# First stage of a transformer encoder layer: k stored once, q stores moved to SyncE's queue, four weight pieces loaded into buffers of h, late adaLN loads on GpSimd's queue, another order of the second chunk's tiles

## The chip, the cores and the metric

The kernel runs on one core of one Trainium2 chip. The metric is the device time of one execution in microseconds; the time of a kernel is the median of several executions. The profile is one more execution, taken by the hardware profiler. Engines are called PE (TensorE, matmuls), DVE (VectorE), ACT (ScalarE), POOL (GpSimd) and SP (SyncE, which only issues transfers here). ACT, POOL and SP can each issue DMAs; an issue stands in that engine's instruction order, and a DMA that waits for something holds up what follows on its engine.

## The reference

One encoder layer (depth 1) over 2048 tokens of width 1024, in float32: windowed attention with 16 query heads over 4 key/value heads of 64, then a gated feed-forward block of width 2816, each between two RMS norms with a conditioning vector c that gives shifts, scales and gates.

```python
mod = (silu(c) @ ada_w[i] + ada_b[i])[:, None, :]
sh1, sc1, g1, sh2, sc2, g2 = jnp.split(mod, 6, axis=-1)
h = rmsnorm(x, mix_norm_pre[i]) * (1.0 + sc1) + sh1
y = windowed_gqa_sink(h, att_w_qkv[j], att_w_o[j], att_sink[j], rel_bias)   # window of 128 to both sides
x = x + g1 * rmsnorm(y, mix_norm_post[i])
h = rmsnorm(x, ffn_norm_pre[i]) * (1.0 + sc2) + sh2
y = swiglu(h, ffn_w_in[i], ffn_w_out[i])
x = x + g2 * rmsnorm(y, ffn_norm_post[i])
```

The first stage, which the change is about, computes `mod`, `h` and the first half of the projection `qkv = h @ w_qkv`.

## The kernel before

**Precision.** A float32 product is made of three matmuls over halves: every operand is split into a high half (ACT: a cast to the matmul type) and a low half (DVE or POOL: operand minus high half), `split`, L149, and `three`, L143, multiplies high by high (L145), high by low (L146) and low by high (L147). So every tile that TensorE reads has two producers, and the second is often the later one.

**Chunks and tiles.** The 2048 tokens are four chunks of 512 (c = 0 to 3). The width of 1024 is eight slices of 128 (k = 0 to 7). The projection has twelve output tiles of 128 columns: 0 to 7 are q (two per key/value head), 8 and 9 are k, 10 and 11 are v, which is computed turned round (`v_tile`, psv). The weight's columns are stored in the order `NORD = [8, 9, 0, 1, 2, 3, 4, 10, 11, 5, 6, 7]`; the first seven (`WAVE`) are the first piece of each slice, `w0_k` (448 KB, loaded as wqkvk_0), the others the second piece, `w1_k` (320 KB, wqkvk_1). Low halves of first pieces are made by DVE, of second pieces by POOL.

**Chunk 0.** TensorE fills its start with 38 matmuls that nobody reads (`keep_busy`). The squares of x are summed over k (`squares0`), the sum over partitions is a matmul with ones (nst), and the inverse root goes to `normed`. Then comes the *first wave*: for every slice k two adaLN columns are loaded and reduced on DVE (`ada_reduce`, L297, a 128x1024 multiply-and-sum: scale 8+k and shift k), the first weight piece is split, x is scaled (L207), and h0_k is made: high half on ACT (L214), low half on DVE (L215). Both need the shift. Seven matmul groups over w0_k follow. Then the tiles are evacuated (`evac`, L219), the second pieces are loaded, and the *second wave* of chunk 0 computes tiles 10, 11, 5, 6, 7.

**Chunks 1 to 3.** Chunk 1 is computed after that, tile by tile, over the second pieces first and the first pieces last. Its squares are summed alternately on POOL and DVE (L186), its norm matmul takes the sum split into halves (L125, L126, in a buffer of the pool `ev`). Between the tiles stand the 24 late adaLN columns (16 to 39; `late_ada`): a load on SP's queue into one of four buffers `raws`, and a reduce on DVE. Chunks 2 and 3 are projected during attention, as *fillers*: a generator (`fill_qkv`) gives one slice of a tile at a time, loads its weights again (wsr), splits them on ACT and POOL (ws), and is asked for a measured amount (`FILL`) after each attention unit.

**Stores and loads.** Every finished q pair is stored in DRAM as four transfers of rows of 256 bytes (q_d, L235; issued by ACT for chunks 0 and 1, by SP for 2 and 3), k twice, once for each half of the partitions (k_d, L243), v once. Attention loads them per chunk and head (`load_qkv`, L457): q, k and v tiles from a pool that lies where the weight pieces were, so that a load waits for the last matmul that reads them.

**Attention.** A unit is 128 queries of one key/value head, four query heads at once, 64 units in all. `scores` (L483): two matmuls for each of four strips (s, L498), then on DVE the bias and the maximum (L501, writes pr and nm), on ACT the exponential with its sum (L503), on DVE a reciprocal (rs, L505), on POOL the scaling (L507). `values` (L513), two units later: transposes of pr (t, L520), split on ACT and DVE (phi, plo), products with v (L525, L526) and the sum of two halves (of, L530). The three buffers pr are cleared once by POOL (L448).

**Who sets the order.** Pools give each tile a buffer and make its next user wait for the readers of the last (`reuse_waits="tile"`). The order of instructions on each engine is set by a scheduler that simulates the program; `tc.issue_after(x)` tells it not to issue what follows before x. The engines then run their own instructions strictly in that order.

## Time and profile before

| | |
|---|---|
| median of 3 runs | 2087.45 us (2087.05 to 2092.54) |
| the profiled execution's own time | 2086.54 us |
| its span on the core | 2084.7 us |
| granted TensorE clock, mean | 0.986 |
| TensorE busy | 2011.4 us, 96% of the span |
| VectorE, ScalarE, GpSimd busy | 1505.5, 994.7, 912.5 us |
| TensorE busy from 0 to 100, 100 to 200 us | 74.2, 87.5 us |
| TensorE busy from 200 to 300 us | 96.41 us |

The span begins with the first and ends with the last instruction of the execution; 1.84 us lie around it. In a row of a timeline the bracket names the idle time of the engine before the instruction and what released it. A wait for several things is put down to the one that came last. The first stage ends at 199 us, with the first scores; attention and its fillers run to about 800 us, the feed-forward block from there to the end.

### The profile page before, as it was taken

How to read it: one execution, taken by the hardware profiler on the slowest of the kernel's cores; microseconds unless marked ns; L12 is line 12 of the kernel's file. 1: busy time of each engine (PE TensorE's matmuls, PEld its weight loads, DVE VectorE, ACT ScalarE, POOL GpSimd, SP SyncE). 2: the span in 40 equal slices, each digit the busy share in tenths (PEclk: the TensorE clock that was granted, in tenths of full speed). 3: DMA queues.
4: the chain of work that ended last, by engine and by line, in shares of the span. 5: the costliest groups of instructions: out<-in, count | busy, mean ns of one | idle time of the engine just before them, and what ended most of it. 6: DMA issues, size and time to landing. Idle time of an engine off the chain costs nothing.

```text
span 2084.7 us, 28731 instructions
## 1 busy us (share of the span) xinstructions
PE 2011.4 (96%) x9416; PEld 1660.3 (80%) x9416; DVE 1505.5 (72%) x2629; ACT 994.7 (48%) x2105; POOL 912.5 (44%) x894
## 2 busy tenths in 40 slices
PE   8698999999999998999999999999999999999998
PEld 5576787888888786888888887888888788888886
DVE  7376677677777668566576698787876598887656
ACT  4233677777777756333333353434433544453222
POOL 0412456543446536455666455545553333344300
PEclk9899999999999999999999999999999999999999
DMA  8699668665556665433643454544533454488763
GB/s 313 194 284 289 199 190 254 177 168 179 179 175 211 206 230 202 141 121 122 228 171 113 154 183 152 198 156 144 200 137 142 161 174 145 156 307 339 258 251 122
DMA packets 257285, 402.69 MB, mean 193 GB/s; under 512 B 84661, under 2 KB 135397, under 8 KB 255088
## 3 DMA queue, kind: packets, MB, share of 16 engines
q1 hardware_dynamic: 216592, 371.41, 52.9%
q10 hardware_dynamic: 39072, 25.18, 3.9%
q0 software_dynamic: 1472, 4.27, 0.5%
q8 instruction: 74, 1.21, 0.2%
q14 instruction: 75, 0.61, 0.1%
HBM read 267.83 MB, written 132.95 MB: 192 GB/s over the span
## 4 chain that ended last, share of the span: by engine, by line
PE 42%; DVE 4%; DMA 1%; issue 1%; POOL 1%; ACT 1%; SPq 0%; DVEq 0%; ACTq 0%; POOLq 0%
PE pc_i L145 8%; PE pc_i L147 8%; PE pc_i L146 8%; PE po L1205 5%; PE po L1206 5%; PE po L1204 5%; DVE z L1245 1%; PE pl L1229 1%; PE pl L1227 1%; PE pl L1228 1%; DMA wiri<-w_in 0%; DVE z L1249 0%; DMA ht<-hd_d_t 0%; DVE z L1209 0%; DVE wo_s L151 0%
## 5 line engine op out<-in xcount | busy, mean ns | idle before, releaser
L146 PE MATMUL pc_i<-ht,ws_i 128*128 128x512 f32 x528 | 207.1, 392 | 1.6 <-DVE ht L151 1.6
L145 PE MATMUL pc_i<-ht,ws_i 128*128 128x512 f32 x528 | 206.2, 391 | 1.8 <-ACT ht L150 1.7
L147 PE MATMUL pc_i<-ht,ws_i 128*128 128x512 f32 x528 | 206.8, 392 | 0.0
L150 ACT CAST wa_i<-wiri 128x512 fp32r<-128x512 f32 x132 | 81.7, 620 | 218.3 <-DMA wiri<-w_in 115.3
L507 POOL TENSOR_SCALAR pr<-pr,rs 128x288 f32<-128x288 f32 (+3 forms) x256 | 126.4, 514 | 116.3 <-DVE rs L505 106.5
L501 DVE CUSTOM_DVE_ANT_0 pr<-s,bias,nsink 128x288 f32<-128x288 f32 (+3 forms) x256 | 124.2, 500 | 57.5 <-PE s L498 47.3
L503 ACT ACTIVATE pr<-pr,nm 128x289 f32<-128x289 f32 (+3 forms) x256 | 135.3, 531 | 55.9 <-DVE nm L501 54.3
L879 POOL TENSOR_TENSOR s_i<-wiri 128x512 f32<-128x512 f32 x44 | 63.9, 1453 | 193.4 <-DMA wiri<-w_in 176.3
L151 DVE TENSOR_TENSOR wa_i<-wiri,wa_i 128x512 fp32r<-128x512 f32 x132 | 127.9, 969 | 22.3 <-ACT wa_i L150 22.0
L151 DVE TENSOR_TENSOR ws_i<-s_i,ws_i 128x512 fp32r<-128x512 f32 x132 | 125.4, 950 | 22.0 <-ACT ws_i L150 21.8
L1209 DVE TENSOR_TENSOR z<-po,z 128x512 f32<-128x512 f32 x164 | 110.6, 684 | 42.2 <-PE po L1206 40.4
L145 PE MATMUL pc_i<-hb,wa_i 128*128 128x512 f32 x352 | 138.1, 392 | 0.0
L147 PE MATMUL pc_i<-hb,wa_i 128*128 128x512 f32 x352 | 137.7, 391 | 0.0
L151 DVE TENSOR_TENSOR plo<-t,phi 128x512 fp32r<-128x512 f32 x184 | 121.9, 683 | 21.9 <-ACT phi L150 21.7
L146 PE MATMUL pc_i<-hb,wa_i 128*128 128x512 f32 x352 | 137.5, 391 | 0.0
L1204 PE MATMUL po<-wo_s,g 128*128 128x512 f32 x320 | 124.8, 393 | 2.0 <-DVE z L1209 1.4
L498 PE MATMUL s<-k,q 128*128 128x288 f32 (+4 forms) x512 | 110.0, 313 | 16.7 <-DMA k<-k_d 10.4
L1205 PE MATMUL po<-wo_s,g 128*128 128x512 f32 x320 | 125.4, 392 | 0.1
L1206 PE MATMUL po<-wo_s,g 128*128 128x512 f32 x320 | 125.2, 391 | 0.0
L520 PE MATMUL t<-ident,pr 128*128 128x128 f32 x736 | 116.0, 274 | 3.1 <-POOL pr L507 2.7
L145 PEld LDWEIGHTS pc_i<-ht,ws_i 128*128 128x128 f32 x528 | 99.5, 188 | 24.1 <-ACT ht L150 2.2
L146 PEld LDWEIGHTS pc_i<-ht,ws_i 128*128 128x128 f32 x528 | 99.5, 188 | 23.6 <-DVE ht L151 2.1
(251 smaller groups left out, 5907.2 us busy)
## 6 DMA issues: line engine op xcount, KB each, us to landing
wiri<-w_in SPq DMA_DIRECT2D x88, 512.0 KB, 4.7
ada<-ada_w SPq DMA_DIRECT2D x40, 512.0 KB, 6.4
wr<-w_out SPq DMA_DIRECT2D x20, 1024.0 KB, 9.1
g<-g_d_t SPq DMA_DIRECT2D x36, 512.0 KB, 5.2
g<-g_d_b SPq DMA_DIRECT2D x35, 512.0 KB, 5.7
q<-q_d SPq DMA_DIRECT2D x16, 1024.0 KB, 6.6
wsr<-w_qkv SPq DMA_DIRECT2D x24, 512.0 KB, 5.7
g<-g_d_t SPq DMA_DIRECT2D x44, 256.0 KB, 3.0
```

The costliest lines, as they stand in the source:

```text
L145: pe.matmul(ps, w[0], h[0], start=first, stop=False)
L146: pe.matmul(ps, w[0], h[1], start=False, stop=False)
L147: pe.matmul(ps, w[1], h[0], start=False, stop=last)
L151: return eng.tensor_tensor(lo, src, f(hi), ALU.subtract).ins
L501: dve.tensor_tensor_reduce(pr[:, i, lo:hi], ps[:, :n], bias[g][:, lo - starts[i]:hi - starts[i]], -1.0, nsink[:, g:g + 1], ALU.add, ALU.mi ...
L503: act.activation(pr[:, i, lo:hi + 1], pr[:, i, lo:hi + 1], AF.Exp, bias=nm[:, i:i + 1], scale=-1.0, accum_out=rs[:, i:i + 1])
L507: pool.tensor_scalar(pr[:, i, lo:hi], pr[:, i, lo:hi], rs[:, i:i + 1], 1.0, ALU.mult, ALU.mult)
L520: pe.transpose(pt[:, i * P:(i + 1) * P], pr[:, i, jj * P:(jj + 1) * P], ident)
L1204: pe.matmul(ps, g[:, 0], w[:, 0], start=i < FRESH and k == 0, stop=False, **on)
L1205: pe.matmul(ps, g[:, 0], w[:, 1], start=False, stop=False, **on)
L1206: pe.matmul(ps, g[:, 1], w[:, 0], start=False, stop=k == m - 1, **on)
L1209: dve.tensor_tensor(y, ps, y, ALU.add)
```

## The change

1. **k is stored once.** A k_d tile has 64 partitions instead of 128 and one store instead of two; `load_qkv` reads it twice, once into each half of the partitions, for the chunk itself and for the neighbours' edges.
2. **q stores of chunks 0 and 1 are issued by SP**, not by ACT.
3. **Four second weight pieces** (k = 0 to 3) are loaded into buffers of the pool `hs`, which holds the h tiles, rather than into `raws`; pool `w2` is opened ahead of `raws`.
4. **The late adaLN columns are loaded on GpSimd's queue**, three per tile of chunk 1 rather than two.
5. **Norms.** The squares of chunk 0 are summed to two tiles rather than four ahead of the matmul; chunk 1's norm takes its sum directly (one matmul, no halves) and is asked for after the first tile of the second wave rather than the second.
6. **First wave.** The reduce of the shift column of slice k is issued after the low half of h0_(k−1).
7. **Chunk 1's tiles** are computed in the order of NORD (8, 9, 0, 1, 2, 3, 4, 10, 11, 5, 6, 7), first pieces first, rather than with the second pieces first. Chunk 2's squares are summed on DVE alone.

```diff
     q_d = [[dram.tile([P, JB * GRP, P], F32, name=f"q_d{c}_{g}") for g in range(KVH)] for c in range(NCH)]
-    k_d = [[dram.tile([P, 2, CH], F32, name=f"k_d{c}_{g}") for g in range(KVH)] for c in range(NCH)]
+    k_d = [[dram.tile([DH, 2, CH], F32, name=f"k_d{c}_{g}") for g in range(KVH)] for c in range(NCH)]
     v_d = [[dram.tile([P, JB, P], F32, name=f"v_d{c}_{g}") for g in range(KVH)] for c in range(NCH)]
...
                     dve.tensor_tensor(sq[k - 1], sq[k - 1], sq[k], ALU.add)
-            self.acc = sq[::2]
-
-        def norm(self, psp, ptag):
-            self.r = rstd_of(lambda name: square_at(), psp, ptag, self.acc, f"a{self.c}", normed[:, 3])
+                if k % 4 == 3:
+                    dve.tensor_tensor(sq[k - 3], sq[k - 3], sq[k - 1], ALU.add)
+            self.acc = sq[::4]
+
+        def norm(self, psp, ptag, direct=False):
+            self.r = rstd_of(lambda name: square_at(), psp, ptag, self.acc, f"a{self.c}", normed[:, 3], direct)
         def h(self, k):
...
                     for i in range(2):
-                        (act if c < 2 else sp).dma_start(q_d[c][g][i * DH:(i + 1) * DH, :, 2 * j * QW:2 * (j + 1) * QW],
+                        sp.dma_start(q_d[c][g][i * DH:(i + 1) * DH, :, 2 * j * QW:2 * (j + 1) * QW],
                                      f(t[j * DH:(j + 1) * DH, i]).rearrange("p b e r -> p b (e r)"))
...
             for j in range(2):
-                for d in range(2):
-                    sp.dma_start(k_d[c][2 * (n - KT) + j][d * DH:(d + 1) * DH], f(t[j * DH:(j + 1) * DH]))
+                sp.dma_start(k_d[c][2 * (n - KT) + j], f(t[j * DH:(j + 1) * DH]))
         else:
...
         sp.dma_start(gains, a["gains"])
-        def ada_load(t, pl):
+        def ada_load(t, pl, q=sp):
             w = pl.tile([P, D], F32, tag="raw", name=f"ada{t}")
-            sp.dma_start(w, a["ada_w"][t])
+            q.dma_start(w, a["ada_w"][t])
             return t, w
...
         wres = {}
+        early = [f(hs.tile([P, 2, CH], F32R, tag="h", name=f"wqkv{k}_1")).rearrange("p a b -> p (a b)") for k in range(KT // 2)]
+
         def w_piece(k, i):
             pl, lo_c, n = (w2, C1, C2) if i else (w1, 0, C1)
-            w = raws.tile([P, D], F32, tag="raw", name=f"wqkv{k}_{i}")
+            if i and k < len(early):
+                w = early[k]
+            else:
+                w = raws.tile([P, D], F32, tag="raw", name=f"wqkv{k}_{i}")
             sp.dma_start(w[:, :n], a["w_qkv"][k, :, lo_c:lo_c + n])
...
                 ada_reduce(*ada_load(8 + k, raws))
-                ada_reduce(*ada_load(k, raws))
+                shift = ada_load(k, raws)
                 w_piece(k, 0)
+            with tc.issue_after(steps[k - 1][1]) if k >= 1 else ExitStack():
+                ada_reduce(*shift)
             dve.scalar_tensor_tensor(coef[:, 0, k:k + 1], mod[:, 8 + k:9 + k], 1.0, gains[:, 0, k:k + 1],
...
         wave.close()
+        w2 = open_pool(pa, "w2", side="right")
         raws = open_pool(pa, "raws", 4, side="right")
-        w2 = open_pool(pa, "w2", side="right")
         for k in range(KT):
...
             for _ in range(min(n, len(left))):
-                waiting.append(ada_load(left.pop(0), raws))
+                waiting.append(ada_load(left.pop(0), raws, pool))
         for i, n in enumerate(NORD[WAVE:]):
             qkv_tile(ch0, n)
-            if i == 1:
-                ch1.norm(psA, "mm")
+            if i == 0:
+                ch1.norm(psA, "mm", True)
             if i >= 1:
...
             if i >= 2:
-                late_ada(min(i - 1, 2), 2)
-        for i, n in enumerate(NORD[WAVE:] + NORD[:WAVE]):
+                late_ada(2 + (i == 4), 2)
+        for i, n in enumerate(NORD):
             qkv_tile(ch1, n)
-            late_ada(2, 2 if left else 0)
+            late_ada(3, 2 if left else 0)
             if i == 0:
                 ch2 = Chunk(2)
-                ch2.squares()
+                ch2.squares((dve, dve))
             if i == 5:
...
         if c > 0:
-            sp.dma_start(f(kk[:, :, :P]), k_d[c - 1][g][:, :, CH - P:])
+            for d in range(2):
+                sp.dma_start(f(kk[d * DH:(d + 1) * DH, :, :P]), k_d[c - 1][g][:, :, CH - P:])
             sp.dma_start(f(v[:, 0]), v_d[c - 1][g][:, JB - 1])
-        sp.dma_start(f(kk[:, :, P:P + CH]), k_d[c][g])
+        for d in range(2):
+            sp.dma_start(f(kk[d * DH:(d + 1) * DH, :, P:P + CH]), k_d[c][g])
         sp.dma_start(f(v[:, 1:1 + JB]), v_d[c][g])
         if c < NCH - 1:
-            sp.dma_start(f(kk[:, :, P + CH:]), k_d[c + 1][g][:, :, :P])
+            for d in range(2):
+                sp.dma_start(f(kk[d * DH:(d + 1) * DH, :, P + CH:]), k_d[c + 1][g][:, :, :P])
             sp.dma_start(f(v[:, 1 + JB]), v_d[c + 1][g][:, 0])
```

What this does to the order of the instructions is shown at three places. On GpSimd, in the first wave of chunk 0, before (`normed` is chunk 1's sum of squares, w1_k the halves of second piece k, wqkvk_1 its load):

```order
L186 TENSOR_TENSOR normed_385<-normed_385,squared_384 128x512 x2
L151 TENSOR_TENSOR w1_0_843<-wqkv0_1_841,w1_0_843 128x640
L151 TENSOR_TENSOR w1_1_848<-wqkv1_1_846,w1_1_848 128x640
L151 TENSOR_TENSOR w1_2_853<-wqkv2_1_851,w1_2_853 128x640
L151 TENSOR_TENSOR w1_3_858<-wqkv3_1_856,w1_3_858 128x640
```

and now:

```order
L186 TENSOR_TENSOR normed_385<-normed_385,squared_384 128x512 x3
L151 TENSOR_TENSOR w1_4_859<-wqkv4_1_857,w1_4_859 128x640
L151 TENSOR_TENSOR w1_0_842<-wqkv0_1_447,w1_0_842 128x640
L294 DMA ada16_1083<-ada_w 128x1024
L151 TENSOR_TENSOR w1_1_846<-wqkv1_1_448,w1_1_846 128x640
```

The third sum, which used to stand behind the fourth piece, stands ahead of all of them, piece 4 comes first, and the first late adaLN load is among them.

On TensorE, from the last matmul of chunk 1 on, before (s are scores, psq2 the filler, chunk 2's projection):

```order
L147 MATMUL psq1_4_1716<-h1_7_1169,w0_7_770 128x512
L498 MATMUL s0_0_0_1812<-k0_0_1798,q0_0_1796 128x256 x2
L498 MATMUL s0_0_1_1817<-k0_0_1798,q0_0_1796 128x224 x2
L145 MATMUL psq2_8_1856<-h2_0_1582,ws2_8_1853 128x512
L146 MATMUL psq2_8_1856<-h2_0_1582,ws2_8_1853 128x512
```

and now (t are transposes of the probabilities):

```order
L147 MATMUL psq1_7_1704<-h1_7_1163,w1_7_874 128x512
L509 MATMUL s0_0_0_1802<-k0_0_1786,q0_0_1784 128x256 x2
L509 MATMUL s0_0_1_1807<-k0_0_1786,q0_0_1784 128x224 x2
L509 MATMUL s0_0_2_1812<-k0_0_1786,q0_0_1784 128x192 x2
L509 MATMUL s0_0_3_1817<-k0_0_1786,q0_0_1784 128x160 x2
L509 MATMUL s1_0_0_1870<-k0_0_1786,q0_0_1784 128x288 x2
L509 MATMUL s1_0_1_1875<-k0_0_1786,q0_0_1784 128x288 x2
L509 MATMUL s1_0_2_1880<-k0_0_1786,q0_0_1784 128x288 x2
L531 MATMUL t0_0_1_1981<-ident_363,pr_0_1778 128x128
```

Chunk 1 ended with a q tile over first pieces (w0) and ends now with one over second pieces (w1). Two tiles of chunk 2's projection used to follow the first scores; now the first of its matmuls stands behind the third strip of the sixth unit (s1_1_2).

On VectorE, late in the second wave of chunk 0, before (ada is a late column's reduce, h1 the low halves of chunk 1):

```order
L297 ISA ada20_1175,mod_358<-ada20_1175,normed_385,adab_359 128x1024
L297 ISA mod_358 128x1
L215 SCALAR_TENSOR_TENSOR h1_0_1045<-x1_0_881,mod_358,h1_0_1045 128x512
L215 SCALAR_TENSOR_TENSOR h1_1_1049<-x1_1_882,mod_358,h1_1_1049 128x512
L215 SCALAR_TENSOR_TENSOR h1_2_1084<-x1_2_883,mod_358,h1_2_1084 128x512
```

and now:

```order
L298 ISA ada20_1168,mod_358<-ada20_1168,normed_385,adab_359 128x1024
L298 ISA mod_358 128x1
L186 TENSOR_TENSOR normed_385<-normed_385,squared_384 128x512
L367 TENSOR_TENSOR e0_v1_958<-psv0_0_908,e0_v1_958 128x2x64
L232 SCALAR_TENSOR_TENSOR eq0_3_1112<-psq0_6_1087,eq0_3_1112 128x16x32
L367 TENSOR_TENSOR e0_v1_958<-psv0_1_975,e0_v1_958 128x2x64
L217 SCALAR_TENSOR_TENSOR h1_4_1116<-x1_4_881,mod_358,h1_4_1116 128x512
```

The reduces of columns 16 to 20 stood ahead of h1_0, whose norm came late; now h1_0 to h1_3 are ahead of 17, and the reduces of 17 to 20 stand ahead of h1_4.

## The prediction

> **What bounds the kernel now.** I read the page first: is one engine the bound of the whole span?
>
> ```profile
> span 2084.7 us, 28731 instructions
> PE 2011.4 (96%) x9416; PEld 1660.3 (80%) x9416; DVE 1505.5 (72%) x2629; ACT 994.7 (48%) x2105; POOL 912.5 (44%) x894
> ```
>
> TensorE works for 2011.4 of 2084.7 us. So the kernel can only win the 73 us in which TensorE stands still, or its time at a low clock. The waits of TensorE say where these are (engine, line and tile, what it waited for: total, times, longest):
>
> ```profile
> PE nsta L127 <- DVE nhla L125: 15.8, 1, 15.8
> PE s L498 <- DMA k<-k_d: 10.4, 1, 10.4
> ...
> PE psq L146 <- DVE h L215: 6.5, 3, 3.3
> ...
> PE psv L147 <- DVE h L215: 2.1, 1, 2.1
> ```
>
> All four lie in the first 200 us, the stage that the change touches. The windows of 20 us place them (length, busy time of PE, PEld, DVE, ACT and POOL, then PEclk, DMA share, GB/s):
>
> ```profile
> 20.00:40.00 20.00, 12.25 (x43) 8.97 (x44) 19.97 (x34) 7.21 (x9) 0.00 (x0) 0.91 1.03 406
> 80.00:100.00 20.00, 4.15 (x15) 3.28 (x14) 3.86 (x11) 2.35 (x9) 0.20 (x1) 0.57 0.84 257
> 180.00:200.00 20.00, 9.63 (x42) 7.65 (x41) 13.70 (x22) 6.50 (x11) 5.87 (x7) 0.80 1.06 333
> 220.00:240.00 20.00, 16.42 (x84) 13.16 (x83) 13.12 (x38) 13.73 (x38) 9.58 (x15) 0.91 0.86 265
> ```
>
> From 20 to 40 VectorE is full and TensorE waits for it. At 80 to 100 nobody works: something is being waited for that is no engine. From 180 on it is a DMA. The timeline of ScalarE, then that of VectorE, gives the chain at 80 (start, length, what; in brackets the idle time before it and its releaser):
>
> ```profile
> 78.77 11.23 ACTq L235 DMA_DIRECT2D q_d<-eq  x4
> 90.04 0.27 ACT L358 CAST e_v<-psv 128x128 fp32r<-128x128 f32 x1 [11.82 <-DMA q_d<-eq]
> ```
>
> ```profile
> 96.14 0.43 DVE L125 CAST nhla<-normed 128x512 fp32r<-128x512 f32 x1 [1.92 <-DMA v_d<-e_v]
> ```
>
> ScalarE issues the q stores itself, and its queue stands behind them: the v evacuations come 11.8 us late, then the v stores, then the buffer in which the norm of chunk 1 is split, and then TensorE, in whose order that norm's matmul comes next. TensorE's timeline shows what the two stalls cost besides:
>
> ```profile
> 96.62 0.80 PE L127 MATMUL nsta<-nhla,ones 128*128 128x512 f32 x1 [15.85 <-DVE nhla L125]
> 97.22 0.63 PE L145 MATMUL psq<-h,w 128*128 128x512 f32 x1
> ...
> 99.78 0.45 PE L145 MATMUL psq<-h,w 128*128 128x512 f32 x1
> ```
>
> ```profile
> 198.95 1.16 PE L498 MATMUL s<-k,q 128*128 128x256 f32 x4 [10.37 <-DMA k<-k_d]
> ...
> 207.30 0.39 PE L145 MATMUL psq<-h,ws 128*128 128x512 f32 x1
> 207.53 0.39 PE L146 MATMUL psq<-h,ws 128*128 128x512 f32 x1
> ```
>
> At full clock these matmuls start 0.234 us apart (207.30 to 207.53); the six from 97.22 to 99.78 took 2.56 us where 1.40 would do, so each long stall drags about 1.2 us of low clock behind it.
>
> **The change part by part.** *q stores on SyncE, norm of chunk 1 direct.* The ScalarE queue no longer stands behind stores, and the direct norm needs no buffer of `ev`. The 15.85 us go, with their 1.2 us: +17.0. What is late next is GpSimd, which makes the low halves of the second weight pieces. A group of instructions (mean ns before the last bar), a row of GpSimd's timeline, one of TensorE's, and one of the DMA issues:
>
> ```profile
> L151 POOL TENSOR_TENSOR w<-wqkv,w 128x640 fp32r<-128x640 f32 x8 | 14.1, 1798 | 0.0
> ```
>
> ```profile
> 57.15 7.51 POOL L151 TENSOR_TENSOR w<-wqkv,w 128x640 fp32r<-128x640 f32 x4
> ```
>
> ```profile
> 69.58 0.28 PE L147 MATMUL psv<-w,h 128*128 128x256 f32 x1
> ```
>
> ```profile
> x<-xT SPq DMA_DIRECT2D x32, 256.0 KB, 4.5
> ```
>
> Before, GpSimd began them at 57.15, 12 us ahead of the end of the first wave (about 69.5, where the psv matmuls set in), and kept ahead. Now all three of GpSimd's square sums of chunk 1 stand ahead of them, and an adaLN load among them, as the order on GpSimd shows (with the change). The third sum needs x1_6, whose buffer is free only when the low half of h0_6 is made (near 54.7 in the new order): 4.5 to land, then a square and two sums, and it ends near 62.8. Then eight times 1.80 and an issue of 0.6 give 77.8 for the last piece. The first wave ends near 66.2 (next point), and until then TensorE has about 6.8 us of work that needs no later piece: −4.7.
>
> *Shift reduces behind the low halves.* The price of one reduce, and the matmul that waited longest for them:
>
> ```profile
> L297 DVE CUSTOM_DVE_ANT_0 ada<-ada,normed,adab 128x1024 f32<-128x1024 f32 x40 | 50.4, 1288 | 0.5 <-DMA ada<-ada_w 0.3
> ```
>
> ```profile
> 35.08 0.80 PE L146 MATMUL psq<-h,w 128*128 128x512 f32 x1 [3.29 <-DVE h L215]
> ```
>
> Three reduces that stood between the norm and the low half of h0_1 no longer do. Run through in the new order, that half is there near 30.4, so that the matmul of 35.08 starts near 30.8; later, at h0_4, VectorE falls behind once, by some 2.6 us, and low clock costs the rest. Net +3.3, the wave ending near 66.2. The 2.1 us in the table of waits, for a low half of chunk 1, go too, since the norm that it hangs on is there 20 us earlier: +2.1.
>
> *k stored once, order of chunk 1's tiles.* The tiles q, k and v of attention lie where the first weight pieces lay. With the old order the last tiles of chunk 1 used these; now the seventh of twelve is the last to use them, so the loads are free about 28 us before attention starts. SyncE's timeline, and the landing time (KB each, median us):
>
> ```profile
> 190.14 0.60 SPq L465 DMA_DIRECT2D k<-k_d  x1
> ```
>
> ```profile
> k<-k_d SPq DMA_DIRECT2D x16, 512.0 KB, 6.9
> ```
>
> Cover of 28 us against 6.9 (twice that, if two 64-partition loads cost double): the 10.37 us go, with 1.1 of low clock: +11.5. The stores that are dropped lay beside other work: nothing.
>
> *The start of attention.* What is late next is the filler. In the order on TensorE (with the change) the scores begin at once, but psq2, chunk 2's projection, comes much later than before. Among the scores of the first five and a half units and the values of three, some 4.25 units of work, there is none of it: its first weights are loaded and split later, the load behind the last q stores of chunk 1 on SyncE, the split behind the fourth unit's scaling on GpSimd. There VectorE sets the pace (groups of 200 to 300, then one of 0 to 200, then the window):
>
> ```profile
> L501 DVE CUSTOM_DVE_ANT_0 pr<-s,bias,nsink 128x288 f32<-128x288 f32 x33 | 16.6, 511 | 9.6 <-PE s L498 9.4
> L501 DVE DVE_READ_ACCUMULATOR2_ANT nm<- 128x1 f32 x45 | 3.7, 81 | 0.0
> L151 DVE TENSOR_TENSOR plo<-t,phi 128x512 fp32r<-128x512 f32 x27 | 18.0, 684 | 4.3 <-ACT phi L150 4.2
> L530 DVE TENSOR_TENSOR of<-o,low 64x512 f32<-64x512 f32 x9 | 6.1, 680 | 2.0 <-ACT low L529 2.0
> L505 DVE RECIPROCAL rs<-rs 128x4 f32<-128x4 f32 x11 | 1.9, 171 | 4.3 <-ACT pr L503 4.2
> L145 PE MATMUL psq<-h,ws 128*128 128x512 f32 x82 | 33.2, 404 | 0.0
> ```
>
> ```profile
> L448 POOL MEMSET pr<- 128x1540 f32 x3 | 4.0, 1387 | 3.1 <-DVE mod L297 3.1
> ```
>
> ```profile
> 200.00:300.00 100.00, 96.41 (x498) 80.06 (x498) 64.45 (x162) 66.64 (x162) 49.41 (x74) 0.97 0.67 192
> ```
>
> A unit takes 4 × 0.59 + 3 × 0.68 + 0.68 + 0.17 = 5.3 us of VectorE, 4.25 units 22.4. The three memsets of the probabilities, which lay under the k wait, now wait for chunk 1's last matmul and put about 3 ahead: 25.4 in all. TensorE has about 15 us to do there (estimate: of 100 us from 200 on it is busy for 96, three times 82 filler matmuls at 0.234 take 57 of them, the other 39 are 11 units of 3.6). It idles 10.4, where 220 to 240 had 3.6: −6.8. I add −1.1 for low clock; were the whole stretch at the 0.43 us pace of 97.22, TensorE's 15 us would be 27, about 2 us more than VectorE needs. [...]
>
> *Late adaLN loads on GpSimd's queue.* The trace has no such load. Its bounds are the same load on SyncE's queue and that plus what GpSimd's queue added to the one transfer that used both:
>
> ```profile
> ada<-ada_w SPq DMA_DIRECT2D x40, 512.0 KB, 6.4
> out<-z POOLq DMA_DIRECT2D x16, 256.0 KB, 6.6
> out<-z SPq DMA_DIRECT2D x8, 256.0 KB, 2.0
> oh<-onehot POOLq DMA_DIRECT2D x1, 65.9 KB, 8.3
> ```
>
> ```profile
> 1855.00:1905.00 50.00, 49.39 (x218) 40.57 (x217) 43.70 (x90) 25.65 (x66) 17.92 (x23) 1.00 0.94 355
> ```
>
> So 6.4 to 11.0 us; I take 11.0, since the stores on that queue, in the window shown, also ran beside a busy VectorE (43.7 of 50). On VectorE four reduces stand ahead of the low halves of h1_4 to h1_7 (the order with the change shows the fourth), needed near 102.8; at 11.0 the first is made near 98.5. 23 loads through four buffers are six rounds of 11.0 + 1.4 + 0.6 = 13 us from about 82, so the last is reduced near 160, before attention starts at 168. No stall, but little slack: −2.0, half of what one more us in a round would take from the slack of 8.
>
> *Sum* against the profiled execution's 2086.54 (span and 1.84 around it; 0.9 under the median): 17.0 − 4.7 + 3.3 + 2.1 + 11.5 − 6.8 − 1.1 − 2.0 = 19.3, 2067 there and **2068** as a median.
>
> **The rivals.** *GpSimd's queue becomes the bound* (the slower side). If a load takes L us, the reduces end at 82 + 6 × (L + 2.0); past 168, from L = 12.3 on, every us costs six, since the last of them stand on VectorE ahead of the first scores' evacuation. L = 13.5 costs 7 (2075), 15.5 all of the gain (2087); from 16.6 the kernel is slower by over 0.3%, at 18 it takes 34 (2102). For it: 66 KB on that queue took 8.3 us. Against: 256 KB took 6.6 beside a VectorE 87% busy. [...] No run here shows a load on that queue.
>
> *Starvation is deeper.* If each unit waits out the whole chain of scores, exponential, GpSimd's scaling and transposes rather than VectorE's sum, the stretch takes some 10 more: 2078. For it: 3.6 us were idle even with fillers.
>
> *The stalls do not go, they move.* k waits for something else, or the Pool pieces come later: one of the big terms, −10, stays: 2078. For it: x1_5 and x1_6 now stand on SyncE's queue ahead of all eight pieces. Against: the waits in the order name only what I counted.
>
> **How the numbers follow.** A measurement of this kernel tells 0.3%, 6.3 us, from nothing. Forecast 0.60 (2058 to 2077, its own bounds: starvation nothing or 8 more); deeper starvation 0.12; stalls moved 0.10; GpSimd's queue 0.18, of which 0.07 at 2075 or so, 0.03 within 0.3%, 0.08 slower. Faster: 0.60 and most of 0.12, 0.10 and 0.07, 0.83; same 0.08; slower 0.09. The range goes from 2058 to 2086.
>
> **What would show it.** In the profile after: no 15.8 and no 10.4 in TensorE's waits; some 5 us waiting for w of GpSimd near 70; a gap-ridden TensorE for 25 us from 168 with waits for VectorE's nm; attention starting near 168 instead of 199. Loads of ada on GpSimd's queue landing in over 13 us, or VectorE waiting for them at 160, would make it wrong; so would later stages that give the time back.

## The result, and the profile after

The changed kernel takes 2076.03 us (median of 4 runs, 2071.01 to 2078.20) where the kernel before took 2089.73 beside it (4 runs, 2087.05 to 2092.54): a ratio of 0.9931, 95% interval 0.9906 to 0.9956. It is faster by 13.7 us, where 19.3 were forecast from the profile. The profiled executions differ by less, 2078.20 against 2086.54 us of their own time, 8.3 us: the one of before was shorter than all four executions beside the changed kernel, the one of after the longest of its four. Keep that in mind for every sum made on two traces below: it accounts for 8.3 us, the medians for 13.7.

The page of the changed kernel opens like this:

```profile
span 2076.4 us, 28772 instructions
PE 2017.2 (97%) x9412; PEld 1660.0 (80%) x9412; DVE 1505.6 (73%) x2632; ACT 992.5 (48%) x2105; POOL 921.8 (44%) x915
```

TensorE stands still for 59.2 us instead of 73.3, 14.1 less. Its busy time is 5.8 longer, with 9412 matmuls recorded where there were 9416. The waits of TensorE in the changed kernel (line and tile, what was waited for: total, times, longest):

```profile
PE s L509 <- DVE nm L512: 7.7, 9, 1.5
PE o L536 <- DVE of L541: 5.1, 5, 2.5
...
PE nsta L121 <- DVE normed L186: 3.4, 1, 3.4
PE t L531 <- POOL pr L518: 3.4, 6, 1.5
PE psq L146 <- DVE h L217: 3.2, 3, 1.7
PE psv L146 <- POOL w L151: 1.8, 2, 0.9
```

The 15.8 us on the norm's halves and the 10.4 on k are gone, and no wait of their size has come up. The windows of 20 us show what stands in their place:

```profile
20.00:40.00 20.00, 18.44 (x78) 14.04 (x76) 20.00 (x33) 7.90 (x11) 0.00 (x0) 1.00 1.03 407
...
60.00:80.00 20.00, 14.81 (x64) 11.81 (x63) 9.38 (x10) 10.96 (x19) 18.35 (x19) 0.74 0.77 241
80.00:100.00 20.00, 20.00 (x117) 17.53 (x117) 18.45 (x35) 7.66 (x18) 3.13 (x6) 1.00 1.01 300
...
160.00:180.00 20.00, 16.31 (x70) 12.61 (x69) 12.29 (x28) 7.20 (x17) 6.21 (x10) 0.96 0.93 264
180.00:200.00 20.00, 16.35 (x97) 13.34 (x97) 16.93 (x56) 15.49 (x43) 9.61 (x25) 0.96 0.87 228
200.00:220.00 20.00, 16.30 (x74) 12.79 (x74) 12.52 (x32) 16.21 (x40) 16.22 (x20) 0.91 0.99 280
220.00:240.00 20.00, 20.00 (x103) 16.70 (x103) 7.51 (x20) 10.00 (x22) 7.29 (x11) 1.00 0.78 237
```

From 80 to 100, where TensorE did 4.15 us of work at a clock of 0.57, it now works all 20 at full clock. The largest part of what is left of the first stage's loss lies in 60 to 80 (5.2 us of idle time, clock 0.74). From 160 to 220 a new loss of 3.7 us per window shows: attention starts without fillers. TensorE's timeline gives the two places:

```profile
67.54 0.39 PE L146 MATMUL psv<-w,h 128*128 128x256 f32 x1 [0.90 <-POOL w L151]
...
69.05 0.56 PE L146 MATMUL psv<-w,h 128*128 128x256 f32 x1 [0.89 <-POOL w L151]
...
74.08 2.08 PE L121 MATMUL nsta<-normed,ones 128*128 128x512 f32 x2 [3.40 <-DVE normed L186]
...
76.17 0.41 PE L146 MATMUL psv<-w,h 128*128 128x256 f32 x1
76.39 0.41 PE L147 MATMUL psv<-w,h 128*128 128x256 f32 x1
...
79.70 0.28 PE L147 MATMUL psv<-w,h 128*128 128x256 f32 x1
79.83 0.28 PE L145 MATMUL psv<-w,h 128*128 128x256 f32 x1
...
172.64 0.40 PE L509 MATMUL s<-k,q 128*128 128x256 f32 x2
...
199.11 0.39 PE L145 MATMUL psq<-h,ws 128*128 128x512 f32 x1
```

Around three gaps of 0.90, 0.89 and 3.40 us the clock is low: the matmuls of 128x256 stand 0.22 us apart (76.17 to 76.39) where 0.13 is the pace a little later (79.70 to 79.83). It is so ahead of the longest gap already: in smaller windows the granted clock is 1.00 from 60 to 68.9, 0.55 from 68.9 to 70.7 and 0.50 from 74.0 to 79.2. From 74 to 79 that costs some 2.5 us more (estimate from these rows). The first scores come at 172.6 and the first filler matmul only at 199.1, 26.5 us later; in the kernel before these were 198.9 and 199.9.

Why the filler is late: SyncE's timeline, then GpSimd's.

```profile
184.34 7.10 SPq L237 DMA_DIRECT2D q_d<-eq  x4
191.50 1.89 SPq L480 DMA_DIRECT2D v<-v_d  x2
193.43 0.44 SPq L552 DMA_DIRECT2D wsr<-w_qkv  x1
```

```profile
199.01 2.38 POOL L151 TENSOR_TENSOR ws<-wsr,ws 128x1024 fp32r<-128x1024 f32 x1
```

The load of the filler's first weights (wsr, 193.43) stands behind chunk 1's last q stores, and the low half (ws, 199.01) behind the scaling of earlier units, as the order had shown.

Four landmarks of TensorE's timeline tell where the difference between the two traces comes from. First stage ends, here with the last matmul of chunk 1's projection: 188.6 before, 172.8 after. First scores: 198.9 and 172.6. Last filler matmul: 452.8 and 435.0. First feed-forward matmul: 780.7 and 772.3. So at the first scores the changed kernel leads by **26.3** us. From there to the last filler matmul it needs 262.4 us instead of 253.9, and the lead falls by **8.5**. From there to the feed-forward it needs 337.3 instead of 327.9, and it falls by **9.4**, to 8.4. From the first feed-forward matmul to the end both take 1304 us, 1304.1 and 1304.0. The 9.4 us are in no term of the prediction. The experiments ask first what each term is worth, and then where these 9.4 come from.

### The profile page after: what moved, and what is told of

Its sections match the earlier page's. It is cut to its first block, busy times and chain, and to the rows that moved or that the text cites. A ratio compares the mean times of both kernels' runs of the same rounds, so it can differ in the third digit from the quotient of the medians.

```text
span 2076.4 us, 28772 instructions
## 1 busy us (share of the span) xinstructions
PE 2017.2 (97%) x9412; PEld 1660.0 (80%) x9412; DVE 1505.6 (73%) x2632; ACT 992.5 (48%) x2105; POOL 921.8 (44%) x915
## 4 chain that ended last, share of the span: by engine, by line
PE 72%; DVE 9%; DMA 9%; ACT 4%; issue 3%; POOL 2%; SPq 1%; DVEq 0%; ACTq 0%; POOLq 0%
PE pc_i L147 12%; PE pc_i L146 12%; PE pc_i L145 12%; PE po L1215 5%; PE po L1216 5%; PE po L1217 5%; PE psq L147 3%; PE psq L145 3%; PE psq L146 3%; PE t L531 2%; PE s L509 2%; PE py L624 1%; PE py L625 1%; PE py L626 1%; PE o L537 1%
## 5 line engine op out<-in xcount | busy, mean ns | idle before, releaser
L509 PE MATMUL s<-k,q 128*128 128x288 f32 (+4 forms) x512 | 114.3, 319 | 9.3 <-DVE nm L512 7.7
```

The lines of the kernel that those rows point to most:

```text
L509: m = pe.matmul(ps[:, :n], qs, kk[:, e, jb * P + lo:jb * P + hi], start=e == 0, stop=e == 1)
```

## The experiments

All are edits of the changed kernel, but for one of the kernel before. This table holds what they are read by (us; landmarks from each kernel's own profile, the last column the median of its runs):

| kernel | first stage ends | first scores | first filler | last filler | feed-forward starts | median |
|---|---|---|---|---|---|---|
| before | 188.6 | 198.9 | 199.9 | 452.8 | 780.7 | 2089.7 |
| after | 172.8 | 172.6 | 199.1 | 435.0 | 772.3 | 2076.0 |
| after, again | 173.4 | 173.3 | 200.0 | 432.9 | 771.0 | 2077.7 |
| old order of tiles | 172.4 | 190.6 | 191.6 | 450.7 | 787.0 | 2091.8 |
| q stores on ScalarE | 181.0 | 180.8 | 214.4 | 445.6 | 784.8 | 2092.7 |
| norm with halves | 182.6 | 182.5 | 184.2 | 442.9 | 773.2 | 2081.2 |
| shift reduces early | 179.4 | 179.2 | 203.0 | 437.4 | 772.2 | 2080.5 |
| adaLN loads on SyncE | 166.6 | 166.5 | 196.6 | 433.2 | 762.9 | 2076.0 |
| four low halves on VectorE | 171.1 | 170.9 | 198.0 | 439.2 | 769.7 | 2077.1 |
| evacuation behind reduces | 172.1 | 176.7 | 187.4 | 441.7 | 769.0 | 2077.7 |
| after, 19.0 pulled | 173.1 | 173.0 | 199.4 | 433.0 | 772.7 | 2074.9 |
| after, 17.0 pulled | 174.2 | 174.0 | 200.5 | 433.6 | 762.5 | 2069.4 |
| before, 19.0 pulled | 189.4 | 197.9 | 198.8 | 456.1 | 788.0 | 2093.3 |
| two of them together | 168.5 | 168.3 | 198.2 | 437.9 | 766.7 | 2071.9 |

From the feed-forward's start to the end of the span the profiles take 1300.2 to 1307.0 us, so a landmark of a single profile says little about differences below some 4 us; the medians do.

### Each part undone

**The old order of chunk 1's tiles.**

```diff
-        for i, n in enumerate(NORD):
+        for i, n in enumerate(NORD[WAVE:] + NORD[:WAVE]):
             qkv_tile(ch1, n)
```

> The change with its seventh point undone: chunk 1's tiles over the second weight pieces first again, all else as changed. Theory (k's loads came free earlier, but the fillers lost their place at the start of attention and took most of it back): TensorE waits again some 10 us for k ahead of the first scores, about 1 us of low clock behind it, and the 8.6 us of extra idling in the 90 us after that are gone again, since psq2 now follows the second strip of scores in the order; net +1 to +4 against the changed kernel, 2077 to 2080. Rival (the tile order is worth its full 11.5 us, the thin start of attention comes from elsewhere, from the late reduces or from SyncE's queue): the k wait is back and the idling stays, 2086 to 2089.

Measured: 2091.8 us (10 runs), ratio to before 1.0009 [0.9994, 1.0024]. The whole gain is gone, more than either side had forecast. A row of the waits of this kernel and its SyncE timeline say why:

```profile
PE s L509 <- DMA k<-k_d: 18.2, 1, 18.2
```

```profile
172.68 2.10 SPq L467 DMA_DIRECT2D q<-q_d  x1
174.87 8.95 SPq L237 DMA_DIRECT2D q_d<-eq  x6
183.92 2.87 SPq L475 DMA_DIRECT2D k<-k_d  x2
```

The first stage still ends at 172.4, and the first load of q is issued at once. But six q stores, which the change has moved to SyncE, stand ahead of the load of k, which is issued 11.2 us later. The wait that was 10.4 us is now 18.2. So this part and the q stores on SyncE aren't two terms that add: without the new order the stores stand in k's way, and what the rest wins is waited away.

**q stores back on ScalarE.**

```diff
-                        sp.dma_start(q_d[c][g]...
+                        (act if c < 2 else sp).dma_start(q_d[c][g]...
```

> The change with only the q stores of chunks 0 and 1 back on ScalarE's queue; chunk 1's norm stays direct. Theory (the 15.8 us wait was made of two things in a row, ScalarE's queue behind stores and the norm's buffer behind v's stores; either one undone leaves most of the gain): TensorE waits at most 6 us in the second wave of chunk 0 beyond the changed kernel's, for high halves of h1 or for banks, 2077 to 2082. Rival (ScalarE's stores alone made the wait): some 12 to 16 us return between 66 and 110, 2088 to 2092.

Measured: 2092.7 us (10 runs), ratio 1.0013 [0.9995, 1.0032]. This costs as much as the rival said, but in two places, of which only the first is the rival's. The waits of TensorE, then ScalarE's timeline:

```profile
PE s L509 <- DVE eq L232: 9.0, 1, 9.0
PE nsta L121 <- DVE normed L186: 7.9, 1, 7.9
```

```profile
69.41 15.47 ACTq L237 DMA_DIRECT2D q_d<-eq  x6
84.92 0.63 ACT L185 ACTIVATE squared<-x 128x512 f32<-128x512 f32 x1 [15.54 <-issue]
...
179.43 5.98 ACTq L237 DMA_DIRECT2D q_d<-eq  x4
185.59 0.60 ACT L231 ACTIVATE eq<-psq 128x512 fp32r<-128x512 f32 x1 [10.66 <-DMA q_d<-eq]
```

At 69 six stores hold up the last square of chunk 1 and with it the norm. At 179 the last stores of chunk 1 hold up the last q evacuation, and the second strip of scores waits 9.0 us for it. In the kernel before the same evacuation was held up as long, by 9.8 us up to 197.75, but under the wait for k, which ended at 198.9; with the new tile order it comes out.

**The norm of chunk 1 with halves, one tile later** (q stores stay on SyncE).

```diff
-            if i == 0:
-                ch1.norm(psA, "mm", True)
+            if i == 1:
+                ch1.norm(psA, "mm")
```

> The change with only chunk 1's norm as before: sum split into halves in a buffer of the evacuations, asked for after the second tile of the second wave; the q stores stay on SyncE's queue. Theory (either one undone leaves most of the gain): the norm's matmul comes after both psv groups and waits 4 to 7 us for the v stores to land; the 3.4 us wait for normed at 71 is gone; 2076 to 2080. Rival (the buffer alone made the wait): 12 to 16 us of it return, 2088 to 2092.

Measured: 2081.2 us (10 runs), ratio 0.9966 [0.9946, 0.9986], 3.5 to 5 us over the changed kernel's two medians (the second is measured below). That is 1 us beyond the theory's range and far from the rival's, but the wait is nearer to the rival's: TensorE waits 10.6 us for nhla, where the theory had 4 to 7. SyncE's timeline and VectorE's in this kernel:

```profile
68.89 13.59 SPq L237 DMA_DIRECT2D q_d<-eq  x8
82.58 5.80 SPq L369 DMA_DIRECT2D v_d<-e_v  x4
```

```profile
90.47 0.43 DVE L125 CAST nhla<-normed 128x512 fp32r<-128x512 f32 x1 [7.64 <-DMA v_d<-e_v]
```

Moved to SyncE, the q stores stand ahead of the v stores there, and a norm that needs a buffer of `ev` still waits for them. It takes both edits to remove the 15.8 us. The first stage ends 9.8 us later than in the changed kernel, and yet only half of that is lost: the fillers start 1.7 us behind the first scores, not 26.5.

**The shift reduces early again.**

```diff
-                shift = ada_load(k, raws)
+                ada_reduce(*ada_load(k, raws))
                 w_piece(k, 0)
-            with tc.issue_after(steps[k - 1][1]) if k >= 1 else ExitStack():
-                ada_reduce(*shift)
```

> The change with only the shift reduces back ahead of the low halves in the first wave. Theory (the 3.3 us gained in the first wave are real and pass through to the end): the two waits of 2 and 3.3 us for low halves of h0 are back between 20 and 40, the first wave ends near 69.5, 2078 to 2081. Rival (behind the first wave TensorE waits for GpSimd's low halves and for normed anyway, 5.2 us between 66 and 75, and these swallow it): the wave ends later but the waits behind it shrink by as much, 2075 to 2077.

Measured: 2080.5 us (5 runs), ratio 0.9959 [0.9940, 0.9978]. TensorE's waits in this kernel:

```profile
PE psq L146 <- DVE h L217: 6.8, 3, 2.6
...
PE psv L146 <- POOL w L151: 5.0, 4, 2.6
```

The time is what the theory said. The first stage ends 6.6 us later than the changed kernel's; 2.3 of these are there at the end of the first wave (67.75 against 65.46, where the psv matmuls set in), the rest comes behind it. Of the 6.6 some 3 to 4 reach the end (2.8 and 4.5 against its two medians).

**The late adaLN loads back on SyncE's queue.**

```diff
-                waiting.append(ada_load(left.pop(0), raws, pool))
+                waiting.append(ada_load(left.pop(0), raws))
```

> The change with only the late adaLN loads back on SyncE's queue, three per tile as changed. Theory (GpSimd's queue is no slower, 6.4 us to landing against 6.4, and its worth is that SyncE's order, which now carries the q stores too, is not held by loads that wait for buffers): SyncE waits for reduces 20 us or more, but k's loads have 20 us of cover and TensorE loses at most 5 us at the start of attention: 2076 to 2081. Rival of the prediction (the queue of GpSimd costs, VectorE's reduces wait for it): faster than changed, 2068 to 2073.

Measured: 2076.0 us (4 runs, of which the profiled one was the fastest at 2069.7), ratio 0.9933 [0.9917, 0.9950]: the same as with GpSimd's queue. SyncE did not wait 20 us for reduces, as the theory had it; from 60 to 200 its waits ahead of these loads come to 9. The first stage is even shorter, by 6.2 us; the window from 60 to 80 and the row of k in this kernel:

```profile
60.00:80.00 20.00, 18.02 (x111) 15.43 (x110) 10.64 (x17) 13.21 (x23) 17.16 (x15) 1.00 0.78 245
```

```profile
PE s L509 <- DMA k<-k_d: 2.4, 1, 2.4
```

That wait for k is not at the first scores: it stands at 208 to 211, for a later head.

Where most of the 6.2 us come from is a row of VectorE's timeline, of the changed kernel and then of this one:

```profile
57.54 0.68 DVE L186 TENSOR_TENSOR normed<-normed,squared 128x512 f32<-128x512 f32 x1
...
69.83 4.20 DVE L186 TENSOR_TENSOR normed<-normed,squared 128x512 f32<-128x512 f32 x1 [0.52 <-ACT squared L185]
```

```profile
69.52 1.14 DVE L186 TENSOR_TENSOR normed<-normed,squared 128x512 f32<-128x512 f32 x1 [0.53 <-ACT squared L185]
```

It is the last sum of chunk 1's squares, on which the norm hangs. The same add takes 0.68 us at 57.54, where GpSimd is idle. In seven profiles with eight low halves in a row on GpSimd and an adaLN load among them (after twice, and five other kernels) it took 4.1 to 4.5. GpSimd's row beside it in the changed kernel:

```profile
64.38 9.10 POOL L151 TENSOR_TENSOR w<-wqkv,w 128x640 fp32r<-128x640 f32 x6
```

The add ends at 74.03, 0.55 us after GpSimd's last low half (73.48). In the other six profiles it ended 0.54 to 0.57 us behind that row. At 69.83, where it started, the fourth of the six low halves (1.5 us each) was running, and it ended behind this one and the two after it. With the loads on SyncE the row of low halves ended as late (60.92 + 12.67 = 73.59), and the add took 1.14. In the kernel before, two such adds took 2.06 and 2.05 beside a row of low halves that ran on. No row shows what held it, and why it ended early there and not here was not tried, so this cause of the 3.40 us is read from the traces and not from an edit that removes it alone.

**Four of the eight low halves on VectorE.**

```diff
-            newest["split"] = split(t[:, 0], t[:, 1], w[:, :n], (dve, pool)[i])
+            newest["split"] = split(t[:, 0], t[:, 1], w[:, :n], (dve, pool)[i * (k % 2)])
```

> The changed kernel with the low halves of second weight pieces 0, 2, 4 and 6 made by VectorE rather than GpSimd, which keeps 1, 3, 5 and 7. Theory (GpSimd's chain of eight halves of 1.8 us behind the sums is the new stall of the first stage): the two waits for w of 0.9 us go, the pieces are there by 71, and TensorE idles and slows 3 to 5 us less between 66 and 80; the wait for normed stays in part; 2071 to 2073. Rival (the sum of chunk 1's squares, whose last slice x1_7 is loaded behind the weight pieces, holds TensorE there whatever GpSimd does): the wait for normed grows from 3.4 to 5 or more as the pieces come earlier, no gain, 2075 to 2077.

Measured: 2077.1 us (4 runs), ratio 0.9933 [0.9906, 0.9960]. TensorE's waits for GpSimd's w are gone, but one of 1.7 us for a piece of VectorE's has come in; the wait for normed falls from 3.4 to 2.0, the first stage ends 1.7 us earlier, and nothing of it reaches the end. The time is the rival's, its reason isn't: the wait for normed did not grow.

**The fillers earlier.** The evacuations of chunk 1 are tied behind the late reduces, so that the buffers of the filler's weights come free earlier.

```diff
-            dve.tensor_tensor_reduce(w, w, cb, ...
+            newest["red"] = dve.tensor_tensor_reduce(w, w, cb, ...).ins
...
         for i, n in enumerate(NORD):
-            qkv_tile(ch1, n)
+            with tc.issue_after(newest["red"]):
+                qkv_tile(ch1, n)
```

> The changed kernel with one rule added for VectorE's order: the evacuation of each tile of chunk 1 is issued behind the adaLN reduces that the program has ahead of it, so that all 40 reduces stand ahead of the last three evacuations and the last two no longer among the scores. Theory (the last reduces hold the buffers in whose place the filler's first weights are loaded, which is why psq2 comes 26 us after the first scores): psq2 starts within 15 us of the first scores, TensorE idles 4 to 7 us less from 160 to 240, 2068 to 2072; nothing waits for the loads on GpSimd's queue, since they land in some 6 us. Rival (the load stands behind chunk 1's last q stores on SyncE's queue whatever the reduces do): psq2 still starts 20 us or more after the first scores, 2074 to 2078.

Measured: 2077.7 us (4 runs), ratio 0.9942 [0.9927, 0.9958]. The first filler stands 10.7 us behind the first scores instead of 26.5, as the theory had it, but two other waits of TensorE have come in, both at the start of attention ("issue" is time in which nothing is waited for that the profile shows):

```profile
PE psq L145 <- ACT ws L150: 4.7, 1, 4.7
...
PE s L510 <- issue: 4.6, 1, 4.6
```

The load of the weights is issued at 178.31 instead of 193.43, behind four of chunk 1's last eight q stores instead of all of them, and SyncE itself waits 3.3 us ahead of it; so the filler, now ordered early, is waited for. What the 4.6 us ahead of the first scores are, the profile doesn't tell. The starvation has changed its place, not its price.

### Where the lead goes

In the table the first stage ends anywhere from 166.6 to 174.2 us for seven kernels with medians of 2069 to 2078, and not in the same order. So the later attention was tested by itself.

**The changed kernel once more**, unaltered, with a second profile.

> The changed kernel once more, unaltered, for a second profile and more times. The question is how much of the 9 us that its attention stage lost against before (from the last filler of chunk 2 and 3 to the first matmul of the feed-forward block it took 337 us, before 328) belongs to the order and how much to the one execution. If it belongs to the order, this stretch is again 335 to 339 us and the median 2076; if to the execution, it comes out near 330 and the profiled time near 2071.

Measured: 2077.7 us (4 runs), ratio 0.9942 [0.9928, 0.9957]. From the last filler matmul to the feed-forward it took 338.1 us, after 337.3 in the first profile. So the long late stretch isn't a chance of one execution; the engines' instructions are in the same order in both.

**Another order of the later units, first stage untouched.** The scheduler is asked for another amount of filler from the 32nd unit on. In the traces TensorE's matmuls are in the changed kernel's order up to 471 us (the first 2200 of 9412), VectorE's instructions up to 474, and the feed-forward's matmuls are in it again, but for three near its start with 19.0. Once with 19.0 and once with 17.0:

```diff
-        fill.pull(FILL, units[max(i - SLACK, 0)].first)
+        fill.pull(FILL if i < 32 else 17.0, units[max(i - SLACK, 0)].first)
```

> The changed kernel with one number altered: from the 32nd unit of the attention on, 19.0 in place of FILL are pulled per unit. The first stage, the first 32 units and the feed-forward are the same as in the changed kernel; only the order of the later units' work differs. In the changed kernel the stretch from the last filler matmul to the first feed-forward matmul takes 337.3 and 338.1 us in two profiles, in the kernel before 327.9, and the runs so far spread from 327 to 339. Theory (the 9.4 us that the late attention gives back belong to the order that the scheduler happens to arrive at): the first scores stay within 1 us of 173, and the sum from first scores to the first feed-forward matmul (599.7 and 597.7 us so far) comes out elsewhere, by 5 us or more in at least one of the two altered orders; total 2068 to 2074 where it falls by that, or above 2080 where it rises. Rival (an earlier start costs the late stretch the same whatever the order, by transfers that collide): the sum stays within 3 us of 598 to 600, total 2075 to 2078.

> The changed kernel with the same number altered the other way: 17.0 in place of FILL from the 32nd unit on. Theory: as in the run with 19.0; first scores within 1 us of 173, the sum from there to the first feed-forward matmul differs by 5 us or more from 598 to 600 in at least one of the two, and the total moves with it. Rival: 598 to 600 within 3 us, total 2075 to 2078.

Measured: 2074.9 us with 19.0 (4 runs; ratio 0.9937 [0.9920, 0.9954]) and 2069.4 with 17.0 (4 runs, 2060.0 to 2071.3; ratio 0.9897 [0.9871, 0.9923]). With 17.0 the interval lies below that of the changed kernel's second measurement and overlaps that of the first. The late stretch in the windows from the last filler matmul to the first of the feed-forward, of the kernel before, the changed one, and the changed one with 17.0:

```profile
452.80:780.70 327.90, 321.38 (x1733) 270.24 (x1732) 233.29 (x635) 236.33 (x625) 152.99 (x249) 0.99 0.60 196
```

```profile
435.00:772.30 337.30, 326.11 (x1736) 271.14 (x1735) 238.24 (x628) 236.23 (x624) 152.84 (x249) 0.99 0.60 188
```

```profile
433.60:762.50 328.90, 321.77 (x1735) 271.68 (x1735) 231.69 (x631) 238.51 (x627) 154.33 (x250) 0.99 0.62 197
```

The same matmuls (but for a few at the edges of the windows) at the same granted clock, and the last kernel has the first stage of the second. With 17.0 the stretch takes 8.4 us less: 4.1 less idle and 4.3 less busy. All of it, and a little more, lies where the order differs: from 2200 matmuls in, at 468 us, to the feed-forward the changed kernel takes 304.0 and 303.7 us in its two profiles, the kernel with 19.0 takes 304.1, and the one with 17.0 takes 294.7. From first scores to the feed-forward it needs 588.5 us, 6.7 above the 581.8 of the kernel before; the changed kernel needs 599.7. The theory holds in one of the two orders (19.0 gives 599.7 again, and a median that can't be told from the changed kernel's), and one was all that it asked for.

**The kernel before, with the same edit.**

```diff
-        fill.pull(FILL, units[max(i - SLACK, 0)].first)
+        fill.pull(FILL if i < 32 else 19.0, units[max(i - SLACK, 0)].first)
```

> The kernel before with the same edit: 19.0 in place of FILL from the 32nd unit on, first stage unaltered. From its first scores (198.9) to the first feed-forward matmul it takes 581.8 us. Theory (order): the first scores stay at 199 within 1 us, and the sum comes out elsewhere, by 5 us or more and rather above (up to 592), since 581.8 is the least of ten orders seen; total 2089 to 2099. Rival (a late start always makes up time): 580 to 585, total 2088 to 2092.

Measured: 2093.3 us (10 runs), ratio 1.0014 [1.0002, 1.0026]. From first scores to the feed-forward it took 590.1 us instead of 581.8, with the first stage unaltered (first scores at 197.9). The order costs something here too: 8 us between two profiles, 3 between the medians. So the kernel before had, by its one profile, the shortest way from first scores to feed-forward of all those in the table; and this profile was one of its shorter executions.

**Two gains of the first stage together**, adaLN loads on SyncE and four low halves on VectorE.

```diff
-            newest["split"] = split(t[:, 0], t[:, 1], w[:, :n], (dve, pool)[i])
+            newest["split"] = split(t[:, 0], t[:, 1], w[:, :n], (dve, pool)[i * (k % 2)])
...
-                waiting.append(ada_load(left.pop(0), raws, pool))
+                waiting.append(ada_load(left.pop(0), raws))
```

> The changed kernel with two steps that each shortened its first stage: the late adaLN loads back on SyncE's queue (first stage ended 6.2 us earlier by itself) and the low halves of four of the eight second pieces on VectorE (1.7 us earlier by itself). Theory (a lead is passed on only in part, since fillers start at about 197 to 200 whatever the first scores do, and the late order decides the rest): first stage ends at 165 to 167, first scores wait up to 4 us for k and the fillers still start at 194 to 200; total 2070 to 2077. Rival (the lead is kept): 2066 to 2069, 8 us under the changed kernel.

Measured: 2071.9 us (4 runs, 2067.3 to 2076.1), ratio 0.9917 [0.9897, 0.9938]. The first stage ends at 168.5, later than with the loads alone (166.6), so these two don't add up. The fillers start at 198.2, and the last filler ends at 437.9, 3 to 5 us later than in the changed kernel in spite of its lead. What it wins, it wins in the late stretch, 328.8 us. The time falls in the theory's range and misses the rival's, though the theory had the first stage end at 165 to 167; its interval overlaps those of the changed kernel, so the two steps aren't shown to win anything.

## Why the prediction was right, and where it was wrong

It forecast 2068 us, 2058 to 2086; 2076 came. The side, the range and most of the steps are right. Of the 8 us between, 2.3 are the kernel before, which ran at 2089.73 beside the changed one and not at the 2087.45 that the sum started from; 5.6 are gain that did not come, 13.7 for 19.3. That 2076 lies in the range is partly luck: the forecast's own part of it, up to 2077, was made wide for a deeper starvation, and the loss came elsewhere. Two of the rivals gave 2078, but the traces speak against both: the two big waits are gone, and the start of attention cost 8.5 us and not some 18. Three of the steps are read from rows of the changed kernel that were not shown yet: SyncE's timeline, the DMA issues (KB each, median us from issue to landing), and the waits of GpSimd.

```profile
144.93 1.50 SPq L475 DMA_DIRECT2D k<-k_d  x2
```

```profile
ada<-ada_w POOLq DMA_DIRECT2D x24, 512.0 KB, 6.4
...
k<-k_d SPq DMA_DIRECT2D x32, 256.0 KB, 7.5
```

```profile
POOL ada L294 <- DVE mod L298: 66.3, 15, 13.6
```

Step by step:

- **q stores and direct norm, +17.0.** Right in cause: the 15.8 us wait is gone. It takes both edits: the norm with halves, with the stores on SyncE, still waits 10.6 us.
- **GpSimd's low halves late, −4.7.** Right in place, short in size, and the larger part has another cause. TensorE waited 0.90 + 0.89 for the pieces, but 3.40 for the norm, whose add on VectorE took 4.20 us beside GpSimd's row of low halves and ended 0.55 behind it, where such an add took 0.68 with GpSimd idle; 5.2 us idle, and the low clock behind it (0.50 from 74.0 to 79.2) some 2.5 more by estimate, 7.7 together.
- **Shift reduces, +3.3, and chunk 1's low half, +2.1.** The first wave ends at 65.5 (66.2 was said). With the two steps above the first stage was to end 17.7 us earlier; it ended 15.8 earlier, by a loss of 7.7 where 4.7 stood, and the early shift reduces by themselves cost 2.3 at the end of the wave and 6.6 at the end of the stage.
- **k and the tile order, +11.5.** Right, with its reason: the wait is gone, and the cover is what was claimed, 28 us. In the changed kernel the first load of k is issued at 144.93 and needed at 172.64, 27.7 us of cover against 7.5 of landing. But the term isn't one of a sum: without the tile order 14 to 16 us are lost, not 11.5, since the q stores on SyncE then stand ahead of k's load and the wait grows to 18.2.
- **Start of attention, −6.8 − 1.1.** Right in size: 7.9 forecast, 8.5 lost between the first scores and the last filler. The stretch without fillers is 26.5 us long, 25.4 were said, and VectorE is busy for 22.0 of it. TensorE is idle for 7.3 in it, not 10.4, but the windows show it idle for another 3.7 from 200 to 220: the size is met by a somewhat different split. No run shows the 1.1 of low clock by itself; in the stretch 0.94 was granted over 19.1 us of work.
- **GpSimd's queue, −2.0, and the rival that it becomes the bound.** The loads landed in 6.4 us there (the row above), as they had on SyncE's queue, with VectorE busy for 52 to 92% of each window from 80 to 160. The 11.0 that were taken were far from it. No run shows the rival's 13.5: the longest of the 24 loads took 10.1. (That no run showed a load on this queue holds for 512 KB loads; the prediction's own row of oh is a load of 66 KB.) Put back on SyncE, the kernel takes the same time. The reckoning of rounds failed as well: the last reduce came at 187.6, not near 160, since the loads waited 66.3 us for buffers that the reduces, late in VectorE's order, had to free; no wait of TensorE's names them.

**The step that failed is the last one, the sum itself**: its terms end with the start of attention, 19.3 us in all, and it was carried to the end as if the rest of attention, whose instructions the change doesn't touch, took as long as before. Up to the last filler it was nearly so in the two profiles, 26.3 less 8.5, or 17.8. Behind it, it wasn't. The prediction had put "later stages that give the time back" among the signs of being wrong, and no price on it. The scheduler, given another first stage, arrived at another order for all of attention, and in this order the stretch from the last filler to the feed-forward takes 9.4 us more in the two profiles; by the medians the loss is smaller (17.8 less 13.7, or 4.1), since the profile of before is one of its short executions.

That the order can do it, and that the earlier start doesn't force it, is shown by the run with 17.0: same first stage, another order, 328.9 us there and 2069.4 in all, close to what the prediction had summed up. In the table four other kernels that start attention about as early (adaLN loads on SyncE, four low halves on VectorE, evacuation behind reduces, two of them together) take 327 to 331 us there as well.

Three things stay open. These four have their last filler late, and from first scores to feed-forward they need 592 to 599 us, little or nothing less than the changed kernel: what they save late they have in part lost before. Of the 9.4 us, about half are idle gaps spread over many small waits for VectorE and GpSimd, and half are busy time of TensorE at the same clock and with the same matmuls, for which no row has an explanation; in the second profile of the changed kernel it is 7.4 idle and 2.8 busy. And how much of a later lead is lost to the order and how much to the fillers' start, at 196 to 201 in nine of the fourteen rows of the table whatever the first scores do, can't be read from these runs for each kernel by itself.

## What to carry to other kernels

Where a scheduler sets the order, a local change redraws the order of everything behind it, and that alone moved the medians of these two kernels by up to 8 us: sum a change's terms at the end of the stage that it touches, then put a range of that size around the rest, and try a few orders of the rest before the change is judged. A wait that is removed uncovers the next one at the same place, so two edits that end in the same wait (here the q stores on SyncE and the order of chunk 1's tiles, or the q stores and the norm) are costed together. Before a stage is made shorter, look at what the next one will then be short of: here the fillers' first weights, which came no earlier.

## What the runs showed of the hardware

- A VectorE add of two 128x512 tiles, 0.68 us where GpSimd was idle, took 4.1 to 4.5 us in seven profiles beside a row of GpSimd's 128x640 subtractions, and ended 0.54 to 0.57 us behind the last of them. It is not always so: beside such a row it took 2.06 and 2.05 in the kernel before. With four of the eight subtractions on VectorE it took 1.5 and 2.4, with the adaLN loads on SyncE 1.1, and 0.69 where it came after GpSimd was done (q stores on ScalarE).
- 512 KB loads issued by GpSimd landed in 6.4 us (3.7 to 10.1), as on SyncE's queue (6.4 before). The issue took GpSimd 0.53 to 0.69 us.
- Behind two gaps of 0.90 and 0.89 us within 2.5 us, 0.55 of the clock was granted, from 68.9 to 70.7, and behind a third gap, of 3.40 us, 0.50 up to 79.2, with a pace of 0.22 us instead of 0.13. With gaps of 0.55, 0.89 and 0.55 in the same place (loads on SyncE) 1.00 was granted from 60 to 80. So here the clock was low behind gaps shorter than the two stalls, 15.85 and 10.37 us, from which the prediction had read its cost.
- k in two loads of 256 KB, one to each half of the partitions, landed in 7.5 us, where one of 512 KB took 6.9: half the partitions at a time did not double it.
